# A windowed-attention stage: the sink as one more column of the scores, and two spilled operands split into high and low parts where they are made

## The chip, the cores and the metric

One core of one Trainium2 chip runs the whole program. The metric is the device time of one execution in microseconds: 1199.33 us before the change, the median of 3 runs (1199.18 to 1199.78).

## The reference

One layer of an encoder over 1024 tokens of width 1024, in float32. The part that matters here:

```python
u = rms_norm(h, norm_mix)
z_pool, q, k, v, g_pool, g_attn = split(u @ w_in)      # 512, 512, 128, 128, 1024, 1024 wide
y_pool = (multiscale_pool(z_pool, w_group) * pool_scale) @ w_pool_branch
# attention: 8 query heads, 2 key heads, blocks of 128, each query block sees 3 key blocks
scores = q k^T / 8 - slope_h * |distance|              # -inf beyond distance 128
m = max(max(scores), sink_h)
p = exp(scores - m)
p = p / (sum(p) + exp(sink_h - m))
y_attn = (p @ v) @ w_attn_branch
h = h + (sigmoid(g_pool) * y_pool + sigmoid(g_attn) * y_attn) @ w_out
```

Then a gated feed-forward layer and a last norm, which the change does not touch.

## The kernel before

Every float32 product is made of three matmuls: an operand is split into a rounded high part and the remainder (`hi`, `lo`), and hi\*hi, hi\*lo and lo\*hi are summed. `split` (L85) makes the high part with a cast on ACT (L87) and the remainder with a subtraction on DVE (L88), or on POOL where it is told to.

The input projection is cut in units of 256 columns; each unit takes seven products, P1 to P7 (a Strassen scheme, `product`, L169), of 12 matmuls of 512 columns. Units `z01`, `z23` feed the pooled branch, `kv` and `q01` the keys, values and the first key head's four query heads, `q23` the second key head's four, and `("g", i)` the gates. A gate is passed through a sigmoid (L301) and written to DRAM (`g_dram`, L302). The units `q23`, g6 and g7 are deferred: their products P2 are kept for the attention stage.

The pooled branch: `windows` (L478) makes window means of z, beside the products of the projection, one piece per product; a small product per half of 512 tokens, a scaled copy on ACT (L512), a write to `p_dram` from the POOL queue (L513). `load_branch` (L569) reads it back in four loads of 512 KB into the `raw` tiles that also hold weights, and splits each into `p_hi` and `p_lo` (ACT, and two remainders each on DVE and POOL).

The second key head's queries are written unsplit (`q_dram`, L311), read back by `load_q` (L603) and split by `use_q` (L339): each tile holds a head's high part in one half of the 128 partitions and its remainder in the other, so that one matmul against the keys does both.

The attention stage is a loop (L722 to L746) over 16 units, that is 2 key heads x 8 query blocks. Step i makes the scores of unit i (`scores`, L621), the transposed probabilities of unit i-3 (`probs`, L656), the values of one before (`values`, L670), and between them `STEPS[i]` branch steps (`branch_step`, L692): 12 matmuls of a branch (first `br<-p_hi`, later `br<-a_hi`), times a gate. `LAST` says how many kept products P2 go before a step. A scores unit, of four heads:

```python
tensor_tensor_reduce(out=s, in0=ps, in1=bias, op0=add, op1=max, accum_out=mx)  # DVE L633, per head
negm = min(-mx, nsink)                                                      # DVE L637
se = negm + sink_b; se = exp(se)                                       # DVE L641, ACT L648
s = exp(s + negm), den = its sum                                          # ACT L645, per head
den = den + se; den = 1 / den                                           # DVE L649, L650
s = s * den                                         # L652: heads 1 and 3 on POOL, the rest on DVE
```

What each engine runs in which order is not the order of the code: a scheduler places the instructions of each engine by its own estimate of times. Each engine then runs its list strictly in that order. Every wait is on semaphores. PSUM has 8 banks of 512 columns, the `s` tile has 3 buffers, a gate's tile 4.

Of the kernel before, what the change touches and what calls it, by code (L numbers as in the profile page):

```python
# [39 lines left out]
P_AT = 1  # L40
# [3 lines left out]
P_POOL = ((0, 2), (1, 0))  # L44
WO_TAIL = 3
AB_POOL = 0
Q_POOL = ((1, 0), (0, 1))
Q_AT = (5, 8)
LAST = (0, 3)
# [4 lines left out]
def encoder_kernel(ctx, tc, x, norm_mix, w_in, w_pool_group, pool_scale, sink, w_pool_branch,  # L54
# [20 lines left out]
    q_dram = dram.tile([2 * P, S], F32, name="q_dram")  # L75
    a_dram = dram.tile([512, S], F32, name="a_dram")
    p_dram = dram.tile([512, S], F32, name="p_dram")
# [191 lines left out]
    big = tc.alloc_tile_pool(name="big", bufs=2, side="right")  # L269
    u_rest = tc.alloc_tile_pool(name="u_rest", bufs=1, side="right")  # L270
# [4 lines left out]
    for name in ("S1", "S2", "S3", "S4", "A22"):  # L275
        combos[name] = tuple(u_rest.tile([P, 4, HALF], F32R, name="%s_%s" % (name, p)) for p in ("hi", "lo"))
# [4 lines left out]
    def in_tile(tag, unit):  # L281
        if tag == "c11" and smp_pool:
            return smp_pool[0].tile([P, HALF], F32, tag="ptl", bufs=3, name="c11")
# [12 lines left out]
    def in_result(unit, row, col, src):  # L296
# [9 lines left out]
        elif unit == "q23":  # L306
            out = src
            if (row, col) == (0, 0):
                out = in_tile("c11", unit)
                nc.scalar.copy(out=out, in_=src)  # L310
            nc.gpsimd.dma_start(out=q_dram[col * P:(col + 1) * P, sl], in_=out)  # L311
        elif unit == "q01":
            use_q(col, sl, src)
# [5 lines left out]
    def use_k(sl, src):  # L319

        scale = HD ** -0.5
# [17 lines left out]
    def use_q(j, sl, src, pool=(0, 0)):  # L339
        for i in range(2):  # L340
            own = slice(i * HD, (i + 1) * HD)
            other = slice((1 - i) * HD, (2 - i) * HD)
            q = qq[2 * j + i]
            nc.scalar.copy(out=q[own, sl], in_=src[own])
            (nc.gpsimd if pool[i] else nc.vector).tensor_tensor(
                out=q[other, sl], in0=src[own], in1=as32(q[own, sl]), op=ALU.subtract)
# [103 lines left out]
    nc.vector.tensor_scalar(out=far, in0=dist, scalar1=float(P), scalar2=NEG, op0=ALU.is_gt, op1=ALU.mult)  # L450
# [6 lines left out]
    wg_raw = zp.tile([P, 4, P], F32, name="wg_raw")  # L457
# [20 lines left out]
    def windows(g):  # L478
# [27 lines left out]
        for half in range(2):  # L506
# [11 lines left out]
    for i, (unit, prod) in enumerate(sequence[:-len(deferred)]):  # L518
# [7 lines left out]
        if prod == "P1" and unit == "kv":  # L526
# [9 lines left out]
            for h in range(4):  # L536
                qq[h] = att.tile([P, S], F32R, tag="qq", bufs=4, name="qq")
# [728 lines left out]
```

## Time and profile before

| what | value |
|---|---|
| median of 3 runs | 1199.33 us |
| the profiled execution, its own time | 1198.78 us |
| its span | 1197.0 us |
| PE busy | 1159.4 us, 97% |
| DVE busy | 858.3 us, 72% |
| ACT busy | 542.7 us, 45% |
| POOL busy | 488.5 us, 41% |
| PE's share of the chain that ended last | 86% (DVE 8%, DMA 2%) |
| attention stage within the span | about 284 to 410 us |

An engine's busy time is the time that its instructions cover. PE's matmuls overlap, so a busy PE may still start them further apart than it could. The chain that ended last is followed back from the last instruction, at each step to what released it.

### The profile page before, as it was taken

The page shows a single profiled execution, that of the slowest core. Times are in us where ns is not written, and L with a number is a line of the kernel's source. Part 1 is how long each engine was busy: PE and PEld are TensorE (multiplying, and loading weights), DVE is VectorE, ACT ScalarE, POOL GpSimd, SP SyncE. Part 2 cuts the span into 40 slices and gives each one's busy share as a digit, 9 for nine tenths or more (in the row PEclk, how much of TensorE's full clock was granted, in tenths as well). Part 3 has the DMA queues.
Part 4 walks back from the last instruction along what each step waited for, and adds up shares of the span by engine and source line. Part 5 has one row for each costly group of instructions (what it writes and reads, how often), then busy time and mean ns, then how long its engine had stood idle before and what let it go on. Part 6 is the DMA issues. An engine that isn't in the chain of part 4 may idle for free.

```text
span 1197.0 us, 15588 instructions
## 1 busy us (share of the span) xinstructions
PE 1159.4 (97%) x5284; PEld 958.9 (80%) x5284; DVE 858.3 (72%) x1339; ACT 542.7 (45%) x1044; POOL 488.5 (41%) x429
## 2 busy tenths in 40 slices
PE   7899999999989999999999999999999999999996
PEld 6788888887778878888778888888888878888885
DVE  6954695756999786539868776777767774665774
ACT  6543345535777644447333332332333344454453
POOL 6833353354554552203445544465455620020230
PEclk9999999999999999999999999999999999999998
DMA  6344134126331565626254544545354457755462
GB/s 211 102 128 146 58 103 144 37 96 220 120 105 59 170 199 186 213 86 194 83 190 171 190 141 140 186 167 166 123 195 158 150 189 259 264 190 196 159 234 100
DMA packets 132372, 186.37 MB, mean 156 GB/s; under 512 B 8450, under 2 KB 87298, under 8 KB 132292
## 3 DMA queue, kind: packets, MB, share of 16 engines
q1 hardware_dynamic: 124372, 158.89, 40.6%
q0 software_dynamic: 6480, 21.24, 4.7%
q10 hardware_dynamic: 1440, 5.24, 1.2%
q8 instruction: 41, 0.67, 0.2%
q14 instruction: 39, 0.32, 0.1%
HBM read 133.70 MB, written 51.64 MB: 155 GB/s over the span
## 4 chain that ended last, share of the span: by engine, by line
PE 86%; DVE 8%; DMA 2%; issue 2%; ACT 1%; POOL 0%; SPq 0%; POOLq 0%; DVEq 0%; ACTq 0%
PE dn L825 17%; PE Y L184 15%; PE X L184 14%; PE Z L184 14%; PE W L184 8%; PE wo L978 7%; PE br L216 2%; PE br L217 2%; PE br L215 2%; DVE wlo L88 1%; PE pt L662 1%; DMA sums<-in_w_ffn_down_dram 1%; PE pv L675 1%; PE tp L376 1%; PE pv L676 1%
## 5 line engine op out<-in xcount | busy, mean ns | idle before, releaser
L87 ACT CAST whi<-raw 128x512 fp32r<-128x512 f32 x378 | 231.1, 620 | 349.9 <-POOL raw L145 84.6
L88 DVE TENSOR_TENSOR wlo<-raw,whi 128x512 fp32r<-128x512 f32 x358 | 320.2, 902 | 67.1 <-ACT whi L87 62.1
L145 POOL TENSOR_TENSOR raw<-raw 128x512 f32<-128x512 f32 x140 | 194.9, 1393 | 239.8 <-DVE wlo L88 205.8
L825 PE MATMUL dn<-wlo,ah 128*128 128x512 f32 x308 | 119.8, 389 | 0.4 <-DVE wlo L88 0.4
L825 PE MATMUL dn<-whi,ah 128*128 128x512 f32 x308 | 117.7, 389 | 1.0 <-ACT ah L87 1.0
L825 PE MATMUL dn<-whi,al 128*128 128x512 f32 x308 | 118.2, 389 | 0.0
L88 DVE TENSOR_TENSOR al<-ab,ah 128x512 fp32r<-128x512 f32 x69 | 48.6, 704 | 67.8 <-ACT ah L87 67.7
L87 ACT CAST ah<-ab 128x512 fp32r<-128x512 f32 x69 | 42.9, 622 | 87.9 <-PE dn L825 87.7
L1050 DVE TENSOR_TENSOR sums<-sums 128x256 f32<-128x256 f32 x88 | 51.1, 580 | 35.9 <-DMA sums<-in_w_ffn_down_dram 33.2
L184 PE MATMUL X<-S_hi,whi 128*128 128x512 f32 x192 | 74.8, 390 | 0.0
L184 PE MATMUL X<-S_hi,wlo 128*128 128x512 f32 x192 | 74.7, 389 | 0.0
L184 PE MATMUL X<-S_lo,whi 128*128 128x512 f32 x192 | 74.7, 389 | 0.0
L184 PE MATMUL Z<-a,whi 128*128 128x512 f32 (+1 forms) x240 | 70.5, 379 | 0.0
L184 PE MATMUL Z<-A_hi,whi 128*128 128x512 f32 x176 | 68.7, 390 | 0.0
L184 PE MATMUL Z<-A_lo,whi 128*128 128x512 f32 x176 | 68.7, 390 | 0.0
L825 PEld LDWEIGHTS dn<-whi,ah 128*128 128x128 f32 x308 | 57.8, 188 | 13.5 <-ACT ah L87 1.4
L184 PE MATMUL Z<-A_hi,wlo 128*128 128x512 f32 x176 | 68.5, 389 | 0.0
L825 PEld LDWEIGHTS dn<-wlo,ah 128*128 128x128 f32 x308 | 57.8, 188 | 12.7 <-DVE wlo L88 0.8
L825 PEld LDWEIGHTS dn<-whi,al 128*128 128x128 f32 x308 | 57.8, 188 | 11.9
L652 POOL TENSOR_SCALAR s<-s,den 128x384 f32<-128x384 f32 (+1 forms) x32 | 38.7, 1220 | 44.4 <-DVE den L650 23.1
L184 PE MATMUL W<-S,whi 128*128 128x512 f32 x176 | 55.6, 396 | 1.0 <-ACT S L87 1.0
L1203 POOL TENSOR_TENSOR o<-o,gain_fin 128x512 f32<-128x512 f32 x8 | 12.4, 1568 | 106.1 <-ACT junk L900 106.1
(268 smaller groups left out, 2832.6 us busy)
## 6 DMA issues: line engine op xcount, KB each, us to landing
ab<-act_dram SPq DMA_DIRECT2D x31, 512.0 KB, 4.0
raw<-in_w_in_dram SPq DMA_DIRECT2D x26, 512.0 KB, 3.8
raw<-in_w_ffn_gate_dram SPq DMA_DIRECT2D x22, 512.0 KB, 3.9
raw<-in_w_ffn_up_dram SPq DMA_DIRECT2D x22, 512.0 KB, 3.8
sums<-in_w_ffn_down_dram SPq DMA_DIRECT2D x44, 256.0 KB, 4.5
wt_dram<-sums SPq DMA_DIRECT2D x22, 512.0 KB, 2.8
act_dram<-sums POOLq DMA_DIRECT2D x44, 256.0 KB, 2.9
raw<-wt_dram SPq DMA_DIRECT2D x20, 512.0 KB, 4.5
```

The source lines that it names most:

```text
L87: ins = nc.scalar.copy(out=hi, in_=src)
L88: (eng or nc.vector).tensor_tensor(out=lo, in0=src, in1=as32(hi), op=ALU.subtract)
L145: nc.gpsimd.tensor_tensor(out=out, in0=x0, in1=x1, op=ALU.subtract)
L184: nc.tensor.matmul(ps, wt[:, c], at[:, k, cols], start=opening and k == 0 and i == 0, stop=k == 3 and i == 2, skip_group_check=not opening)
L215: nc.tensor.matmul(ps, wh, xh, start=first, stop=False)
L216: nc.tensor.matmul(ps, wh, xl, start=False, stop=False)
L217: nc.tensor.matmul(ps, wl, xh, start=False, stop=last)
L652: (nc.gpsimd if i in POOL_HEADS else nc.vector).tensor_scalar(out=s[:, i, :W], in0=s[:, i, :W], scalar1=den[:, i:i + 1], scalar2=None, op0 ...
L825: nc.tensor.matmul(ps[t], at[:, ts], wt, start=opening and k == 0 and e == 0, stop=k == nk - 1 and e == 2, skip_group_check=not opening)
L978: nc.tensor.matmul(ps[t], at[:, k, ts], wt, start=k == 0 and e == 0, stop=k == KT - 1 and e == 2)
L1050: nc.vector.tensor_tensor(out=out, in0=in0, in1=in1, op=op)
L1203: nc.gpsimd.tensor_tensor(out=o[t][:, :HALF], in0=o[t][:, :HALF], in1=gain3[:, :HALF], op=ALU.mult)
```

## The change

- The sink becomes one more column of the scores. All scores change their sign (the scale of the keys, the bias and the mask are negated), the reduction takes the minimum, and its start value is the negated sink instead of a constant; so `negm` comes out of the reduction. POOL copies the negated sinks into column W of `s`; the exponential reads W + 1 columns with a scale of -1, and its sum holds the sink's term. L637, L641, L648 and L649 are gone.
- The pooled branch is split when it leaves PSUM (ACT cast with the scale, DVE remainder), both parts are written (`p_dram` has two), and four loads of 1 MB from the ACT queue bring them straight to where the products read them, in the tiles of the projection's operands S1 and S2, which are free by then.
- The second key head's queries are split where they are made too (`q_dram` has two parts), and sixteen loads of 128 KB of 64 partitions each bring the parts to their places. The query tiles are cut in halves of 512 tokens, eight buffers; the second head's tiles reuse the first's.
- The kept products P2 stand before steps 0 (two) and 1 (one) instead of three before step 1. The tiles of `pth` and `ptl` have 4 buffers instead of 3.

```diff
-LAST = (0, 3)
+LAST = (2, 1)
-Q_AT = (5, 8)
+Q_AT = (5, 9)
...
         elif unit == "q23":
-            out = src
             if (row, col) == (0, 0):
-                out = in_tile("c11", unit)
-                nc.scalar.copy(out=out, in_=src)
-            nc.gpsimd.dma_start(out=q_dram[col * P:(col + 1) * P, sl], in_=out)
+                hi, lo = [in_tile("c11", unit).bitcast(F32R) for _ in range(2)]
+            else:
+                hi, lo = in_tile("c11", unit).bitcast(F32R), src.bitcast(F32R)
+            split(src, hi, lo)
+            for i, part in enumerate((hi, lo)):
+                nc.gpsimd.dma_start(out=q_dram[i, col * P:(col + 1) * P, sl], in_=as32(part))
...
-            p = zp.tile([P, HALF], F32, tag="p", bufs=2, name="p")
-            nc.scalar.activation(out=p, in_=ps, func=AF.Copy, scale=psc[:, g:g + 1])
-            nc.gpsimd.dma_start(out=p_dram[g * P:(g + 1) * P, sl], in_=p)
+            hi, lo = [zp.tile([P, HALF], F32, tag="p", bufs=3, name="p").bitcast(F32R) for _ in range(2)]
+            split(ps, hi, lo, scale=psc[:, g:g + 1])
+            for i, part in enumerate((hi, lo)):
+                nc.gpsimd.dma_start(out=p_dram[i, g * P:(g + 1) * P, sl], in_=as32(part))
+    def load_p(half):
+        for i, part in enumerate(("hi", "lo")):
+            p_split[half, i] = t = u_sums.tile([P, 4, HALF], F32R, tag="S%d_%s" % (half + 1, part), bufs=1, name="p_" + part)
+            with tc.issue_after(sigmoids[-1]):
+                nc.scalar.dma_start(out=as32(t),
+                                    in_=p_dram[i, :, half_of(half)].rearrange("(t p) q -> p t q", p=P))
...
+    def load_q(row):
+        for h in range(4):
+            qq[4 + h, row] = q = att.tile([P, HALF], F32R, tag="qq", bufs=8, name="qq")
+            for part, rows in enumerate(rows_of(h % 2)):
+                nc.sync.dma_start(out=as32(q[rows]), in_=q_dram[part, h * HD:(h + 1) * HD, half_of(row)])
...
+        s = sm.tile([P, 4, 3 * P + 8], F32, tag="s", bufs=3, name="s")
+        nc.gpsimd.tensor_copy(out=s[:, :, W], in_=nsink[:, hs])
...
-            nc.vector.tensor_tensor_reduce(out=s[:, i, :W], in0=ps[:, :W], in1=bias[:, i, c0:c0 + W], scale=1.0,
-                                           scalar=NEG, op0=ALU.add, op1=ALU.max, accum_out=mx[:, i:i + 1])
-        ins = nc.vector.scalar_tensor_tensor(out=negm, in0=mx, scalar=-1.0, in1=nsink[:, hs], op0=ALU.mult,
-                                             op1=ALU.min)
-        nc.vector.tensor_tensor(out=se, in0=negm, in1=sink_b[:, hs], op=ALU.add)
+            ins = nc.vector.tensor_tensor_reduce(
+                out=s[:, i, :W], in0=ps[:, :W], in1=bias[:, i, c0:c0 + W], scale=1.0,
+                scalar=nsink[:, 4 * g + i:4 * g + i + 1], op0=ALU.add, op1=ALU.min, accum_out=negm[:, i:i + 1])
...
-                ins = nc.scalar.activation(out=s[:, i, :W], in_=s[:, i, :W], func=AF.Exp, bias=negm[:, i:i + 1],
-                                           accum_out=den[:, i:i + 1])
-        nc.scalar.activation(out=se, in_=se, func=AF.Exp)
-        nc.vector.tensor_tensor(out=den, in0=den, in1=se, op=ALU.add)
+                ins = nc.scalar.activation(out=s[:, i, :W + 1], in_=s[:, i, :W + 1], func=AF.Exp, scale=-1.0,
+                                           bias=negm[:, i:i + 1], accum_out=den[:, i:i + 1])
...
-        if i == P_AT:
-            with behind(P_AT - 1, (0,)):
-                load_branch(p_dram, p_hi, p_lo, pool_t=P_POOL)
```

The lists move where the stage begins. On DVE, before, from the first unit's last reduction on (`sc` is a bank of scores, `p_lo` the pooled branch's remainder):

```order
L633 ISA s,mx<-sc,bias 128x256
L633 ISA mx 128x1
L637 SCALAR_TENSOR_TENSOR negm<-mx,nsink 128x4
L88 TENSOR_TENSOR p_lo<-raw,p_hi 128x2x512 x2
L641 TENSOR_TENSOR se<-negm,sink_b 128x4
L649 TENSOR_TENSOR den<-den,se 128x4
L650 RECIPROCAL den<-den 128x4
L633 ISA s,mx<-sc,bias 128x384
```

And in the change, at the same place:

```order
L646 ISA s,negm<-sc,bias,nsink 128x256
L646 ISA negm 128x1
L656 RECIPROCAL den<-den 128x4
L658 TENSOR_SCALAR s<-s,den 128x256 x2
L646 ISA s,negm<-sc,bias,nsink 128x384
```

Between the first unit's last reduction and the second unit's first, four instructions with a remainder pair of the pooled branch among them are gone.

On ACT, before, at the start of the stage (the sigmoids of the kept products are L301, the exponentials L645):

```order
L301 ACTIVATE s_2411<-s_2411 128x512
L645 ACT_TABLE_LOAD
L645 ACTIVATE s,den<-s,negm 128x256 x4
L648 ACTIVATE se<-se 128x4
L87 CAST whi<-raw 128x512 x2
L301 ACT_TABLE_LOAD
L301 ACTIVATE c_2606<-Z 128x512
L301 ACTIVATE c_2627<-Z 128x512
L310 COPY c_2646<-Z 128x512
L87 CAST whi<-raw 128x512 x2
L87 CAST pth<-pt 128x512 x2
L645 ACT_TABLE_LOAD
```

And in the change, where the loads of the pooled branch's two parts stand too:

```order
L301 ACTIVATE t_2512<-t_2512 128x512
L526 DMA p_hi<-p_dram 128x4x512
L526 DMA p_lo<-p_dram 128x4x512
L84 CAST whi<-raw 128x512
L301 ACTIVATE s_2474<-s_2474 128x512
L84 CAST whi<-raw 128x512 x2
L301 ACTIVATE c_2597<-Z 128x512
L301 ACTIVATE s_2454<-s_2454 128x512
L526 DMA p_hi<-p_dram 128x4x512
L526 DMA p_lo<-p_dram 128x4x512
L84 CAST whi<-raw 128x512
L301 ACTIVATE c_2618<-Z 128x512
```

All sigmoids now stand before the first exponential; the first half's two loads are behind the sigmoid of unit g7's P7, the second half's behind that of its P4.

On SP, before, the loads ahead of the stage (`raw` is the shared tile of weights and spilled parts):

```order
L573 DMA raw<-p_dram 128x2x512 x3
L302 DMA g_dram<-t_2469 128x512
L302 DMA g_dram<-s_2431 128x512
L573 DMA raw<-p_dram 128x2x512
L579 DMA sg<-g_dram 128x512 x4
L104 DMA raw<-in_w_pool_branch_dram 128x4x256
```

And in the change, at the same place:

```order
L101 DMA raw<-in_w_pool_branch_dram 128x4x256 x3
L302 DMA g_dram<-t_2512 128x512
L302 DMA g_dram<-s_2474 128x512
L101 DMA raw<-in_w_pool_branch_dram 128x4x256
L302 DMA g_dram<-c_2597 128x512
L302 DMA g_dram<-s_2454 128x512
L101 DMA raw<-in_w_attn_branch_dram 128x4x256
```

The branch's weights took the place of the spilled parts in the `raw` tiles; the gates' loads moved behind.

On PE, of the change, the list from that P4 (its matmuls are `Y`) to the second branch step runs: 12 `Y`, 13 `Z` (the kept products), 8 `sc` of 256 columns, 12 `Z`, 8 `sc` of 384, 12 `br` (first half of the tokens), 8 `sc`, 8 `pt`, 12 `br` (second half). From there on it repeats 8 `sc`, 12 `pt`, 4 to 6 `pv`, 12 `br`, where before most of these groups were cut in pieces of one to six.

## Rows read from the trace of the kernel before

**Rows 1.** Windows: length, PE, PEld, DVE, ACT, POOL busy (instructions), clock, DMA share, GB/s.

```profile
280.00:420.00 140.00, 132.02 (x683) 111.56 (x682) 126.56 (x337) 99.16 (x243) 75.14 (x58) 0.99 0.41 134
420.00:440.00 20.00, 18.78 (x79) 14.17 (x78) 16.36 (x21) 9.83 (x17) 8.90 (x6) 1.00 0.57 181
284.00:410.00 126.00, 118.02 (x616) 99.91 (x615) 118.81 (x323) 93.34 (x233) 66.73 (x51) 0.99 0.37 122
360.00:410.00 50.00, 50.00 (x274) 43.79 (x273) 45.18 (x132) 35.17 (x91) 22.45 (x18) 1.00 0.31 96
```

**Rows 2.** Timeline of PE, one undisturbed step: start, length, engine, line, instruction, count.

```profile
365.83 0.33 PE L631 MATMUL sc<-kkh,qq 128*128 128x384 f32 x1
...
367.25 1.47 PE L662 MATMUL pt<-ident,s 128*128 128x128 f32 x12
368.48 0.48 PE L675 MATMUL pv<-pth,vv 128*128 128x512 f32 x1
...
369.49 0.39 PE L215 MATMUL br<-p_hi,whi 128*128 128x512 f32 x1
...
372.22 0.33 PE L631 MATMUL sc<-kkh,qq 128*128 128x384 f32 x1
```

**Rows 3.** Waits of PE, 280 to 440 us: us in total, times, longest.

```profile
PE br L215 <- ACT whi L87: 1.6, 1, 1.6
PE sc L631 <- ACT c L301: 1.3, 1, 1.3
```

**Rows 4.** Groups of DVE, 284 to 410 us: busy us, mean ns, idle before.

```profile
L345 DVE TENSOR_TENSOR qq<-raw,qq 64x512 fp32r<-64x512 f32 x4 | 6.1, 1554 | 0.1
L641 DVE TENSOR_TENSOR se<-negm,sink_b 128x4 f32<-128x4 f32 x16 | 5.3, 329 | 0.1
...
L637 DVE SCALAR_TENSOR_TENSOR negm<-mx,nsink 128x4 f32<-128x4 f32 x16 | 4.6, 289 | 0.1
L88 DVE TENSOR_TENSOR p_lo<-raw,p_hi 128x1024 fp32r<-128x1024 f32 x2 | 4.6, 2318 | 0.0
...
L649 DVE TENSOR_TENSOR den<-den,se 128x4 f32<-128x4 f32 x16 | 3.5, 218 | 1.8 <-ACT se L648 1.7
```

**Rows 5.** The instructions of L641 (ns min/median/max), and POOL's timeline at 299 us.

```profile
L641 DVE TENSOR_TENSOR se<-negm,sink_b x16: 135/158/2706, 293.5 to 402.7; 128x4 f32<-128x4 f32 x16
...
299.39 2.51 POOL L88 TENSOR_TENSOR wlo<-raw,whi 128x512 fp32r<-128x512 f32 x2
```

**Rows 6.** Windows around the start of the stage, and the busiest one for DMA.

```profile
296.00:300.00 4.00, 3.15 (x15) 3.06 (x15) 3.93 (x15) 3.34 (x7) 3.97 (x5) 0.70 0.47 177
300.00:304.00 4.00, 4.00 (x19) 3.37 (x18) 4.00 (x8) 3.70 (x9) 1.91 (x2) 0.87 0.49 189
...
280.00:300.00 20.00, 17.11 (x80) 14.36 (x78) 16.44 (x41) 14.51 (x26) 11.70 (x8) 0.94 0.73 246
...
404.00:408.00 4.00, 4.00 (x20) 3.26 (x19) 1.50 (x6) 2.50 (x6) 1.44 (x2) 1.00 1.03 349
```

**Rows 7.** DMA issues: queue, count, KB each, median us from issue to landing.

```profile
p_dram<-p POOLq DMA_DIRECT2D x8, 256.0 KB, 3.2
raw<-p_dram SPq DMA_DIRECT2D x4, 512.0 KB, 3.7
```

**Rows 8.** Windows over the stretch in which the pooled branch is made.

```profile
140.00:200.00 60.00, 60.00 (x264) 49.34 (x263) 47.88 (x66) 28.93 (x47) 30.02 (x25) 1.00 0.35 115
160.00:180.00 20.00, 20.00 (x90) 16.39 (x89) 19.85 (x30) 10.64 (x19) 10.66 (x7) 1.00 0.37 126
200.00:280.00 80.00, 80.00 (x360) 66.38 (x360) 48.92 (x68) 35.18 (x63) 30.91 (x24) 1.00 0.27 83
```

**Rows 9.** Single lines' instructions, ns min/median/max: remainder with a scale, two small POOL operations.

```profile
L328 DVE SCALAR_TENSOR_TENSOR kkl<-Z,kkh x4: 683/688/694, 206.8 to 210.4; 64x512 fp32r<-64x512 f32 x4
...
L476 POOL MEMSET z<- x4: 105/113/115, 58.0 to 140.0; 128x8 f32 x4
...
L908 POOL TENSOR_TENSOR rstd<-ms,mhalf x16: 549/569/1463, 494.2 to 1189.0; 128x1 f32<-128x1 f32 x16
```

More of the change, by code (lines that the diff above doesn't have):

```diff
@@ L39 @@
 FILL = (128, 480)
-P_AT = 1
 BIAS_AT = 5
@@ L269, in encoder_kernel @@
     big = tc.alloc_tile_pool(name="big", bufs=2, side="right")
+    u_sums = tc.alloc_tile_pool(name="u_sums", bufs=1, side="right")
     u_rest = tc.alloc_tile_pool(name="u_rest", bufs=1, side="right")
@@ L275, in encoder_kernel @@
     for name in ("S1", "S2", "S3", "S4", "A22"):
-        combos[name] = tuple(u_rest.tile([P, 4, HALF], F32R, name="%s_%s" % (name, p)) for p in ("hi", "lo"))
+        pool = u_sums if name in ("S1", "S2") else u_rest
+        combos[name] = tuple(pool.tile([P, 4, HALF], F32R, name="%s_%s" % (name, p), tag="%s_%s" % (name, p), bufs=1)
+                             for p in ("hi", "lo"))
     st = tc.alloc_tile_pool(name="st", bufs=1, side="right")
@@ L337, in use_v, with use_q, rows_of @@
             split(pv[:, :, g], vv[0][:, 4 * row:4 * row + 4, g, 0], vv[0][:, 4 * row:4 * row + 4, g, 1])
-    def use_q(j, sl, src, pool=(0, 0)):
+    def use_q(j, row, src):
         for i in range(2):
[L341 to L346, printed above, removed]
+            own, other = rows_of(i)
+            q = qq[2 * j + i, row]
+            nc.scalar.copy(out=q[own], in_=src[own])
+            nc.vector.tensor_tensor(out=q[other], in0=src[own], in1=as32(q[own]), op=ALU.subtract)
+    def rows_of(i):
+        return slice(i * HD, (i + 1) * HD), slice((1 - i) * HD, (2 - i) * HD)
     def in_product(unit, prod, **kw):
@@ L535, in encoder_kernel @@
                 kkl[g] = att.tile([P, S], F32R, tag="kkl", bufs=2, name="kkl")
-            for h in range(4):
-                qq[h] = att.tile([P, S], F32R, tag="qq", bufs=4, name="qq")
+            for row in range(2):
+                for h in range(4):
+                    qq[h, row] = att.tile([P, HALF], F32R, tag="qq", bufs=8, name="qq")
         in_product(unit, prod)
+        if (unit, prod) == (deferred[-1], "P7"):
+            load_p(0)
         ahead(1)
@@ L562, in encoder_kernel @@
     pp = tc.alloc_tile_pool(name="pp", bufs=1, side="right")
-    p_hi, p_lo = [pp.tile([P, 4, S], F32R, name=n) for n in ("p_hi", "p_lo")]
     merged = []
@@ L601, in behind @@
             yield
-    def load_q(h):
-        raw = raw_tile()
-        nc.sync.dma_start(out=raw, in_=q_dram[h * P:(h + 1) * P, :])
-        for i in range(2):
-            qq[4 + 2 * h + i] = (att2 if h == 0 else att).tile([P, S], F32R, tag="qq", bufs=2 if h == 0 else 4,
-                                                             name="qq")
-        for half in range(2):
-            use_q(2 + h, half_of(half), raw[:, half_of(half)], Q_POOL[h])
+    def load_q(row):
+        for h in range(4):
+            qq[4 + h, row] = q = att.tile([P, HALF], F32R, tag="qq", bufs=8, name="qq")
+            for part, rows in enumerate(rows_of(h % 2)):
+                nc.sync.dma_start(out=as32(q[rows]), in_=q_dram[part, h * HD:(h + 1) * HD, half_of(row)])
     sm = tc.alloc_tile_pool(name="sm", bufs=1)
@@ L707, in branch_step @@
             if j == 0:
[L708 removed]
+                load_branch(a_dram, *brs[1:], half)
             held["w"] = weights()
[L710 removed]
+            pool, hi, lo = brs[0], brs[1][:, :, sl], brs[2][:, :, sl]
         gt = load_gate(pool, b * KT + j, half)
[L712 removed]
+        ps = branch(held["w"], hi, lo)
         if b == 0:
@@ L743, in encoder_kernel @@
             if i in Q_AT:
-                with behind(i - 1):
-                    load_q(Q_AT.index(i))
+                load_q(Q_AT.index(i))
             scored.append(scores(g, n, biases[g]))
```

59 lines of the change are left out of this document (25 added, 34 removed).

## The prediction

> **What bounds the kernel now.** I looked first for stretches in which PE is not busy, because the time table shows PE busy for 97% of the span and the chain that ended last is mostly PE. The windows show them in one place: PE is full from 140 to 280 us [rows 8], and between 280 and 420 us it is busy for 132.02 of 140 us [rows 1]. In the same place DVE is at its limit: 118.81 of 126 us between 284 and 410 [rows 1]. PE's waits there [rows 3] name ACT and DVE as releasers, nine short ones of at most 1.6 us, of which two are shown. The change touches nothing else in the kernel but the stretch in which the pooled branch and the queries are made, so the question is how much PE time this stage loses, and how much comes back.
>
> Idle time alone undercounts the loss, because modelled matmuls overlap and because a matmul at half clock counts as busy. So I count what the stage's matmuls need when nothing disturbs them. One such step [rows 2]: 8 score matmuls of 384 columns start within 1.42 us (0.1775 each), 12 transposes within 1.23 (0.1025), 12 matmuls of 512 columns within 2.73 (0.2275), and 4 value matmuls take 1.01, which is 0.1 more than four of 512 columns, so about 0.08 once per unit. For 256 columns I take two thirds of 384, 0.12. The window of 140 us holds 683 matmuls [rows 1]; by the program 176 of them are transposes and 125 are scores as the trace has them (96 of 384, 29 of 256), and 382 have 512 columns. Needed: 382 x 0.2275 = 86.9, 96 x 0.1775 = 17.0, 29 x 0.12 = 3.5, 176 x 0.1025 = 18.0, and 15 x 0.08 = 1.2; together 126.6. **PE loses 13.4 us in 280 to 420.** The next 20 us hold 79 matmuls of 512 columns, 18.0 us of need: 2.0 us lost, where the last attention block goes to DRAM and back before the branch product can read it. Part of the loss is the clock: it stood at 0.70 and 0.87 in two windows of 4 us [rows 6], right after PE had idled, that is 1.2 + 0.5 = 1.7 us of work not done.
>
> **The change part by part.** *The sink column.* DVE loses three small instructions in each of 16 units: 5.3 + 4.6 + 3.5 = 13.4 us [rows 4]. ACT loses 16 small exponentials. The reduction keeps its shape and the exponential reads one column more; nothing for both (were each of the 64 exponentials and 64 reductions 10 ns longer, 0.6 us on engines that then have room). POOL gains 16 copies of 128x4. No row shows one; the nearest are a fill of 128x8 at 0.113 us and a power of 128x1 at 0.569 [rows 9], so 1.8 to 9.1 us, on an engine that is busy for 66.73 of 126 [rows 1]. I take 1.8, since a copy is nearer to the fill. The copy waits until the transposes have left that buffer of `s`, and POOL's normalisations stand behind it; the lag of three units covers that. If the cover went, a step would wait for a copy of up to 0.57 us, 9 us in all.
>
> *The pooled branch.* In the attention stage DVE loses two remainders of 1024 columns, 4.6 us [rows 4], the first of them in front of the second unit's scores, as the lists show; ACT and POOL lose their shares of it. Where the branch is made, DVE gains 8 remainders with a scale, at the 0.688 us of such an instruction of the same length [rows 9]: 5.5 us; ACT keeps its 8 casts. POOL issues 8 writes more. DVE is idle for 12.1 us of 140 to 200 [rows 8], but only for 0.15 between 160 and 180. What hides the 5.5 us are weights split ahead in four buffers; from both sides 0 and 5.5 us of PE, and I take 0.3, by the nearest row: PE is full at 160 to 180 even though DVE is.
>
> *The loads.* Four loads of 1 MB replace four of 512 KB. From the P7 sigmoid to the first use of the second half PE has some 16.5 us of work: 13.0 from the end of the `Y` matmuls (37 of 512 columns 8.4, scores 0.96 + 1.42 + 1.42, transposes 0.82), and about 3.5 before. In 280 to 300 the DMA moved 246 GB/s, 4.9 MB [rows 6], of which one load of 0.5 MB was the pooled branch; that leaves 4.4 in 20 us, 3.6 in 16.5. The new loads add 4.2 MB. The most that any window shows is 349 GB/s [rows 6]. If the four loads go first they need 12.0 us and are in time: 0. If all else goes first, 7.8 MB take 22.4 us: 5.9 us late. Three of the branch's four weight loads (1.5 MB) now stand earlier on the SP queue, as the raw tiles are free: 6.3 MB, 18.1 us, 1.6 late, and with the landing of the last part I take 2.0.
>
> The Trainium skill speaks against the move here, "DMA: Bandwidth & Descriptors", section "Issuing engines are not separate DMA queues": transfers from several engines' queues share the same 16 DMA engines and interleave, so a second queue saves only issue time. No run here has yet shown two queues side by side. With the page's ceiling of about 358 GB/s per core (its section "Specifications") the estimate for 6.3 MB would be 17.6 us, 1.1 late, and the time 0.9 us lower.
>
> *The queries.* In the stage DVE loses 4 remainders, 6.1 us [rows 4], POOL 4 and ACT 8. Where the queries are made, 3 casts and 3 remainders of 512 columns are added; at 0.69 us on DVE they lie in 200 to 280, where DVE is busy for 48.92 of 80 [rows 8]: nothing, and 2.1 us at most without that cover. The fourth pair falls in the stage: 0.7 us of DVE. The 16 small loads stand on the SP queue behind the scores that free their tiles, and gate loads stand behind them. Three units or more pass before the first use of each, so only the gates matter: four gate tiles are in flight, and I put nothing.
>
> *The order.* With all sigmoids before the first exponential, ACT's table is loaded once instead of three times, and PE has two kept products to run while ACT makes the first exponentials, which is where the two waits shown are [rows 3].
>
> **The sum.** DVE in the stage: 118.8 - 13.4 - 4.6 - 6.1 + 0.7 = 95.4 us, against some 113 us of PE work in the same 126 us (126 less the 13 lost). DVE was 6 us over PE's need; now it is 18 under. So PE becomes the bound of this stage and the waits go, except: the pooled loads 2.0; the steps without a branch product, where PE has 4 us of work and DVE 6 (95.4 / 16), 1.0 after what the lag of three covers; 0.3 in the stretch before. The tail keeps 1.7 of its 2.0, because the way to DRAM and back is unchanged. 13.4 - 2.0 - 1.0 - 0.3 + 0.3 = **10.4 us less**. The profiled execution took 1198.78, so 1188.4; it stood 0.55 under the median, so 1188.9 for the median.
>
> **The rivals.** *The pooled loads are late, and the clock falls.* For: 246 GB/s moved there already. Against: the SP queue's gate loads wait for buffers and come late. Price: 5.9 instead of 2.0, and the 1.7 us of clock that came with the idle time before: gain 10.4 - 3.9 - 1.7 = 4.8, time 1194.5.
>
> *DVE is relieved by less.* The small additions of the sink took 158 ns in the median, but 329 in the mean, and one took 2706 while POOL ran two instructions for 2.51 us [rows 5]. So about half of their time was waiting behind POOL, and the next DVE instruction may do that waiting instead. If all of the 24.1 us removed were so, 12 us would stay: DVE 107 of 113. Then half of the waits stay, 6.7, and with the same losses the gain is 3.7: 1195.6.
>
> The Trainium skill has the rule for this, "SBUF — State Buffer", section "Who interferes with whom": a DVE instruction with two SBUF inputs and a GpSimd (POOL) one that reads SBUF exclude each other for the whole instruction. The row of 2706 ns agrees; by the rule the reductions and remainders that read PSUM would not wait in their place, which speaks against this rival.
>
> *The stretch before pays for it: slower.* The pooled branch's `p` tiles are now three, used by pairs, so every remainder writes a tile whose DMA of the half before must have landed, 3.2 us from its issue [rows 7]. DVE is strictly in order: if it waits there, weights and the projection's sums stand behind it. With eight waits of 3.2 and 5.5 us of work, less DVE's 12.1 us of idle time, PE loses 19 us, the stage gives 10.7 back, and the time is 1207.6. It decides the sign from 2.2 us per wait on. Against: the halves lie a product (2.7 us) or more apart, and the lists put other DVE work between.
>
> *The stage is held by its chain, not by DVE.* Scores, exponential, normalisation and transposes follow each other through four engines, and the waits only change their names: about 1199. Against: between 360 and 410, where neither branch nor queries are split, the same chain runs with PE busy throughout [rows 1].
>
> **How the numbers follow.** Forecast 56%, with a range of its own from 1184.9 (all of the 13.4 and half of the tail) to 1193. Late loads 22%, less relief 12%, slower 6%, no change 4%. The range 1184.5 to 1195.5 holds the first two and half of the third. A difference of 0.2%, 2.4 us, is about what a measurement of this kernel can tell from none. Faster by more: 0.56 + 0.22 and half of the third, 0.85. Slower 0.07, the rest 0.08.
>
> **What would show it.** Right: DVE at 93 to 98 us over the stage, PE's waits on DVE gone between 310 and 355, steps of 6.4 to 6.9 us from the third on, one table load. The pooled loads show as PE `br` waiting for a DMA, in the first two branch steps alone. Wrong: DVE below 100 us and the waits still there, with ACT or POOL as releasers; or PE no longer full between 140 and 200 us.

## The result: 1192.17 us, and the profile after

| | before | after |
|---|---|---|
| median of the runs side by side | 1199.55 us | 1192.17 us (1190.59 to 1192.71) |
| ratio | | 0.9936, 95% interval 0.9918 to 0.9953 |
| profiled execution, its span | 1198.78, 1197.0 us | 1191.99, 1190.1 us |

The change is 7.4 us faster; 10.4 were forecast, and the time lies in the range.

To see where the 6.9 us of span came from, fixed points are better than windows of fixed times, because later work moves into those. I take the last matmul of the projection (`Y`) and the last one of the attention branch (`br<-a_hi,wlo`). From PE's timeline of the kernel before, and then of the change (start, length, line, instruction):

```profile
283.77 0.39 PE L184 MATMUL Y<-A_hi,wlo 128*128 128x512 f32 x1
...
453.50 0.39 PE L217 MATMUL br<-a_hi,wlo 128*128 128x512 f32 x1
```

```profile
285.11 0.39 PE L181 MATMUL Y<-A_hi,wlo 128*128 128x512 f32 x1
...
446.04 0.39 PE L214 MATMUL br<-a_hi,wlo 128*128 128x512 f32 x1
```

The **stage** between them took 169.73 us and takes 160.93: 8.80 less. The way to its start is 1.34 us longer, and from its end to the end of the span it is 743.50 before and 744.06 after, 0.56 longer. -8.80 + 1.34 + 0.56 = -6.90. The windows of just this stage, before and then after (columns as in [rows 1]):

```profile
284.16:453.89 169.73, 160.53 (x803) 133.76 (x802) 155.75 (x372) 113.28 (x266) 93.12 (x69) 0.99 0.44 141
```

```profile
285.50:446.43 160.93, 157.16 (x802) 133.61 (x802) 138.67 (x319) 99.80 (x235) 85.58 (x80) 0.99 0.53 170
```

PE does nearly the same work (803 and 802 matmuls recorded), but not the same matmuls: 7 more of 512 columns and 6 fewer short scores fall into the stage before, since the lists place some of each ahead of its start. By the prices of the prediction the stage's matmuls need 154.4 us before and 153.5 in the change. So PE loses 15.4 us in it before and 7.4 after: 8.0 of the 8.80 are won, and 0.9 is work that now stands ahead of the start, which is most of the 1.34. DVE is busy for 17.1 us less in it, ACT 13.5, POOL 7.5, and the DMA moves more. The windows of the change that answer to [rows 1, 6, 8]:

```profile
280.00:420.00 140.00, 136.98 (x718) 117.95 (x717) 115.40 (x291) 89.50 (x217) 72.59 (x73) 0.99 0.51 165
420.00:440.00 20.00, 19.25 (x83) 14.89 (x82) 18.22 (x23) 11.14 (x19) 9.05 (x7) 1.00 0.71 230
284.00:410.00 126.00, 122.98 (x656) 106.36 (x655) 107.40 (x279) 83.09 (x207) 66.71 (x68) 0.99 0.52 168
...
140.00:200.00 60.00, 59.75 (x262) 48.79 (x261) 55.13 (x75) 28.13 (x46) 30.90 (x32) 1.00 0.39 139
...
288.00:292.00 4.00, 4.00 (x23) 3.43 (x23) 2.42 (x10) 3.67 (x8) 3.16 (x3) 1.00 1.06 400
292.00:296.00 4.00, 4.00 (x21) 3.53 (x20) 3.12 (x9) 3.12 (x10) 2.87 (x3) 1.00 1.06 407
296.00:300.00 4.00, 2.84 (x19) 2.45 (x17) 3.13 (x12) 1.90 (x6) 3.73 (x5) 1.00 1.06 400
300.00:304.00 4.00, 2.58 (x8) 2.05 (x9) 2.40 (x7) 2.88 (x10) 1.41 (x3) 0.77 0.86 325
304.00:308.00 4.00, 4.00 (x22) 3.60 (x21) 1.71 (x5) 1.59 (x4) 2.95 (x3) 0.80 0.22 77
```

PE's idle time is now nearly all at one place, 296 to 308 us, and the waits of 280 to 440 (us in total, times, longest) name it. Of the nine before, beside the two of [rows 3]:

```profile
PE pv L675 <- DVE merged L714: 1.3, 1, 1.3
PE pt L662 <- DVE ptl L88: 1.2, 1, 1.2
PE pv L675 <- DVE mx L633: 1.2, 1, 1.2
PE br L215 <- ACT a_hi L87: 0.9, 1, 0.9
PE sc L631 <- DVE at L683: 0.7, 1, 0.7
PE sc L631 <- DVE qq L345: 0.4, 1, 0.4
PE br L216 <- DVE a_lo L88: 0.3, 1, 0.3
```

In the change those on `a_hi` and `a_lo`, in the tail, are left of them; the late load is new, and two more of 0.2 us are not shown:

```profile
PE br L213 <- DMA p_lo<-p_dram: 2.6, 1, 2.6
PE br L212 <- ACT a_hi L84: 0.5, 1, 0.5
PE br L213 <- DVE a_lo L85: 0.3, 1, 0.3
```

The second branch step waits for the remainders of the second half; then the granted clock is 0.77 and 0.80 in two windows of 4 us, that is for a part of them 1.2 instead of 2.4 GHz; (0.23 + 0.20) x 4 = 1.7 us of work not done. The DMA issues of 276 to 312 us (queue, count, KB each, median us to landing; the second `p_lo` alone also took 14.7):

```profile
p_hi<-p_dram ACTq DMA_DIRECT2D x2, 1024.0 KB, 9.8
p_lo<-p_dram ACTq DMA_DIRECT2D x2, 1024.0 KB, 14.7
```

In the groups of DVE, 284 to 410 us, the small instructions, the branch's two remainders and the queries' four [rows 4] are gone, but the reduction has become longer. Before, and then now:

```profile
L633 DVE CUSTOM_DVE_ANT_0 s<-sc,bias 128x384 f32<-128x384 f32 x48 | 24.6, 549 | 0.1
L633 DVE CUSTOM_DVE_ANT_0 s<-sc,bias 128x256 f32<-128x256 f32 x16 | 5.8, 413 | 0.0
```

```profile
L646 DVE CUSTOM_DVE_ANT_0 s<-sc,bias,nsink 128x384 f32<-128x384 f32 x48 | 27.3, 609 | 3.2 <-PE sc L645 3.2
...
L646 DVE CUSTOM_DVE_ANT_0 s<-sc,bias,nsink 128x256 f32<-128x256 f32 x16 | 6.8, 477 | 0.0
```

And the added instructions, POOL's copy and the remainder with a scale (ns min/median/max), beside [rows 9]:

```profile
L639 POOL COPY s<-nsink x16: 180/191/536, 286.9 to 385.0; 128x4 f32<-128x4 f32 x16
...
L88 DVE SCALAR_TENSOR_TENSOR p<-gm,psc,p x8: 732/741/752, 152.3 to 199.3; 128x512 fp32r<-128x512 f32 x8
```

### The profile page after: what moved, and what is told of

Read it like the earlier page. It is cut to its first block, busy times and chain, and to the rows that moved or that the text cites. A ratio compares the mean times of both kernels' runs of the same rounds, so it can differ in the third digit from the quotient of the medians.

```text
span 1190.1 us, 15576 instructions
## 1 busy us (share of the span) xinstructions
PE 1154.1 (97%) x5284; PEld 955.8 (80%) x5284; DVE 854.1 (72%) x1297; ACT 531.2 (45%) x1017; POOL 485.0 (41%) x451
## 4 chain that ended last, share of the span: by engine, by line
PE 80%; DVE 10%; DMA 4%; issue 3%; ACT 1%; POOL 1%; SPq 0%; POOLq 0%; DVEq 0%; ACTq 0%
PE dn L827 17%; PE X L181 13%; PE Y L181 13%; PE Z L181 12%; PE wo L980 7%; PE W L181 7%; DVE wlo L85 3%; PE br L213 2%; PE br L214 2%; PE br L212 2%; DMA sums<-in_w_ffn_down_dram 2%; DMA p_lo<-p_dram 1%; PE pt L668 1%; PE pv L681 1%; PE pv L682 1%
## 5 line engine op out<-in xcount | busy, mean ns | idle before, releaser
L827 PEld LDWEIGHTS dn<-whi,ah 128*128 128x128 f32 x308 | 57.8, 188 | 13.5 <-ACT ah L84 1.4
```

The source lines that it names most:

```text
L827: nc.tensor.matmul(ps[t], at[:, ts], wt, start=opening and k == 0 and e == 0, stop=k == nk - 1 and e == 2, skip_group_check=not opening)
```

## The experiments

Beside the times I give each run's stage, read between the same two matmuls as above; it repeats better than the time (the change in two profiled executions 160.93 and 160.67, its improved version 157.96 and 157.95), while the rest of the span scatters: from the stage's end on it took 742.6 to 744.9 us in these profiles. Every other kernel's stage is one profiled execution. Since not quite the same matmuls lie between the two fixed ones everywhere, the table also gives what PE loses in it, that is the stage less its matmuls by the prices of the prediction, and DVE's busy time in it, all in us:

| kernel | stage | PE's loss | DVE busy |
|---|---|---|---|
| before | 169.73 | 15.4 | 155.75 |
| sink_only | 168.88 | 14.5 | 149.32 |
| q_only | 170.17 | 15.8 | 146.68 |
| q_last21 | 163.98 | 10.3 | 141.86 |
| p_only | 167.58 | 14.1 | 147.84 |
| the change | 160.93 | 7.4 | 138.67 |
| change_side | 160.67 | 7.2 | 139.79 |
| no_sink | 160.85 | 7.4 | 143.54 |
| last03 | 162.95 | 8.8 | 141.76 |
| buf3 | 165.25 | 11.8 | 137.99 |
| p_early | 159.18 | 5.1 | 140.63 |
| early_nosink | 160.00 | 6.0 | 143.99 |
| early_const | 157.96 | 3.9 | 137.26 |
| early_side | 157.95 | 3.7 | 137.29 |

### The parts one by one

**sink_only**: the kernel before with the sink as a column, and nothing else.

```diff
-            mx = reduce(ps + bias, max); negm = min(-mx, nsink); se = exp(negm + sink_b); den = den + se
+            negm = reduce(ps + bias, min, start nsink); column W of s = nsink; the exponential reads W + 1
```

> The kernel before with the sink column alone (signs, seed, copy, exponential); pooled branch and queries are loaded and split as before. Theory A (DVE's length of the attention stage decides, each part counts by what it takes off DVE): the three small instructions take 13.4 us off DVE, the reductions get 64 x 0.06 = 4 us longer, so 9 us net of the 118.8; PE's waits from 310 to 355 us shrink, those at 292 to 297 stay, because the pooled remainders still stand in front of the second unit: 2 to 4 us less than before, 1195.5 to 1197.5. Rival B (the pooled branch and the queries made nearly all of the loss): within 1 us of before. Rival C (the small instructions, which also wait behind POOL, made it): 7 us less, as the whole change.

1197.86 us, ratio 0.9981 (0.9970 to 0.9992), stage 168.88. DVE busy for 111.99 of 284 to 410 us instead of 118.81. It helps a little by itself: 2.3 us in the medians, as theory A had it, but only 0.9 of PE's loss in its profiled stage; the rest is not found there.

**no_sink**: the change with the sink as before.

> The changed kernel with the old sink: maximum with a constant start, three small DVE instructions and one exponential more per unit, no copy. Theory A: DVE gains 13.4 - 4 = 9 us in the stage and is again near PE's need, so some short waits come back in steps that carry no branch product and around the second bias: 1 to 3 us more than the changed kernel, 1193.2 to 1195.2. Rival B: within 1 us of the changed kernel. Rival C: back to before, 1198 to 1199.

1192.86 us, ratio 0.9938 (0.9921 to 0.9956), stage 160.85: the change's own. DVE has 113.09 us of work between 284 and 410 instead of 107.40 and the time is the same. **On top of the other parts, with the late load, the sink column is worth nothing.** Something is traded all the same: PE's wait for `p_lo` is 0.9 us here instead of 2.6, and waits on DVE have come, 1.1 for `merged` and 0.6 for `s`. What the column is worth with the load in time, the last runs show.

**q_only**: the kernel before with the queries split where they are made.

```diff
-            nc.gpsimd.dma_start(out=q_dram[col * P:(col + 1) * P, sl], in_=out)
+            split(src, hi, lo)
+            for i, part in enumerate((hi, lo)):
+                nc.gpsimd.dma_start(out=q_dram[i, col * P:(col + 1) * P, sl], in_=as32(part))
```

> The kernel before with the queries alone split where they are made and loaded in sixteen pieces into halved tiles. Theory A: 6.1 us less on DVE, in two bursts at 325 and 347 us; the waits next to them (0.4 and 1.3 us, and their restarts) go: 1 to 3 us less than before, 1196.5 to 1198.5. Rival B': the queries cost nothing where they were: within 0.7 us of before.

1201.56 us, ratio 1.0013 (1.0003 to 1.0023), stage 170.17: slower, a miss. The waits of 325 to 350 us are gone as expected, but new ones stand at the start. ACT's, DVE's and PE's timelines there:

```profile
294.97 1.14 ACT L87 CAST whi<-raw 128x512 fp32r<-128x512 f32 x2 [4.16 <-DMA raw<-in_w_pool_branch_dram]
```

```profile
296.13 6.26 DVE L618 SCALAR_TENSOR_TENSOR bias<-dist 128x384 f32<-128x384 f32 x4 [9.06 <-ACT whi L87]
```

```profile
296.83 0.44 PE L632 MATMUL sc<-kkh,qq 128*128 128x384 f32 x1 [2.85 <-ACT c L301]
302.79 0.69 PE L632 MATMUL sc<-kkh,qq 128*128 128x384 f32 x1 [4.58 <-DVE mx L634]
```

ACT stands behind a late load of weights; DVE stands for 9.06 us in front of the first write of `bias`, and the bias then takes 6.26 us for four instructions whose median is 552 ns, while POOL runs remainders from SBUF (2.82 us from 295.67, 2.49 from 299.01). The Trainium skill, "SBUF — State Buffer", section "Who interferes with whom", says that a DVE instruction with two SBUF inputs and a POOL one reading SBUF exclude each other; this row agrees with it. As what released the `bias` the row names ACT's cast; in the list as built the `bias` waits for an earlier sigmoid and for three DMA queues, and the write `g_dram<-s`, issued at 291.39, took 4.6 us to land, so it is the likelier one.

**q_last21**: q_only with the kept products in the change's places.

```diff
-LAST = (0, 3)
+LAST = (2, 1)
```

> The kernel before with the queries' split alone (as q_only), but with the kept products two before step 0 and one before step 1. Theory M (q_only lost only by an accident of the lists at the start: ACT stood 4.2 us behind a late load of branch weights, DVE 9.1 us behind ACT, and PE 7.4 us behind both; the queries' own worth, the waits of 325 to 350 us, is there and shows as soon as PE has other work): 1195 to 1197.5, with under 3 us of PE waits between 290 and 306 us. Rival N (one split alone cannot pay, because the other still fills DVE at the start): 1199 to 1202, with 5 us or more of PE waits there.

1195.30 us, ratio 0.9952 (0.9935 to 0.9969), stage 163.98. The time is as theory M said, its bound on the waits is not: PE still waits 3.0 and 2.8 us there. DVE stood nearly as long as in q_only:

```profile
293.16 1.97 DVE L618 SCALAR_TENSOR_TENSOR bias<-dist 128x384 f32<-128x384 f32 x4 [8.46 <-DMA g_dram<-s]
```

So rival N's time falls, though its waits came: the queries pay without the pooled branch, 5.75 us of stage together with the order (5.1 of PE's loss). That it is the two kept products which cover DVE's stand is argued from their place.

**p_only**: the kernel before with the pooled branch split where it is made, loaded ready, and the kept products at (2, 1).

```diff
-            nc.scalar.activation(out=p, in_=ps, func=AF.Copy, scale=psc[:, g:g + 1])
-            nc.gpsimd.dma_start(out=p_dram[g * P:(g + 1) * P, sl], in_=p)
+            split(ps, hi, lo, scale=psc[:, g:g + 1])
+            for i, part in enumerate((hi, lo)):
+                nc.gpsimd.dma_start(out=p_dram[i, g * P:(g + 1) * P, sl], in_=as32(part))
```

> The kernel before with two parts of the change: the pooled branch split where it is made and loaded ready, and the kept products in the change's places (two before step 0, one before step 1). The queries and the sink stay as before. Theory E (the pooled branch carries the gain: without its loads, casts and remainders at the start of the stage PE's waits of 290 to 320 us shrink, and the queries' remainders later only cost the waits that the kernel before had at 325 to 350): 1193 to 1195, that is 5 to 7 us less than before. Rival F (the two splits must come together, since either alone leaves DVE above 100 us in the stage and the lists only put the waits elsewhere, as the queries alone did): 1198 to 1201, no more than 2 us from before.

1197.92 us, ratio 0.9982 (0.9967 to 0.9996), stage 167.58, at the edge of rival F. It trades one wait for another: 3.2 us for `p_lo`, where casts and remainders were waited for.

With the order, then, p_only gives 2.15 us of stage (1.3 of PE's loss) and q_last21 5.75 (5.1), and both together 8.88 (8.0, no_sink). The sum is not a test of whether the two splits help or hinder each other: the order is counted in both runs, and both have three buffers for `pth` and `ptl` where no_sink has four, which buf3 shows to count for more than the difference. Of the two runs the queries' gives more, also with the stand of DVE that it has and the change has not. How the 5.75 divides between the order and the queries stays open: without it the queries gave nothing (q_only), and the order alone on the kernel before was not run.

### What the change does beside its parts

**last03**: the change with the kept products where they were.

```diff
-LAST = (2, 1)
+LAST = (0, 3)
```

> The change with the kept products where they were before: three before step 1, none before step 0. Theory G (the kept products before step 0 fill the time in which the first exponentials and the table load run; without them PE waits there, and after the wait it runs at half clock): 2 to 4 us more than the change, 1194.5 to 1196.5, with a PE wait on ACT or DVE of 1.5 us or more between 288 and 298 us. Rival H (the start is bound by the pooled loads, so work moved behind them gives them time: the wait for p_lo shrinks as the other grows): within 1 us of the change, 1191.5 to 1193.

1193.94 us, ratio 0.9951 (0.9934 to 0.9968), stage 162.95, 2.0 longer than the change's (1.4 of PE's loss). The time lies between theory G's 1194.5 and rival H's 1193. No wait is where theory G put one: the only long one is 1.8 us for `p_lo`, less than the change's 2.6 as rival H had it, and the rest of the loss is spread.

**buf3**: three buffers for the transposed probabilities instead of four.

```diff
-            hi = smp.tile([P, 512], F32R, tag="pth", bufs=4, name="pth")
-            lo = smp.tile([P, 512], F32R, tag="ptl", bufs=4, name="ptl")
+            hi = smp.tile([P, 512], F32R, tag="pth", bufs=3, name="pth")
+            lo = smp.tile([P, 512], F32R, tag="ptl", bufs=3, name="ptl")
```

> The change with three buffers instead of four for the high and low parts of the transposed probabilities. Theory O (these buffers are a silent part of the gain, and the reason why the two splits together give more than the sum of them apart, which ran with three): 1194.5 to 1197, with PE's transposes or scores waiting for DVE ptl or ACT pth at 1 us or more in all. Rival P (the splits themselves make the gain): within 1 us of the change.

1197.51 us, ratio 0.9979 (0.9969 to 0.9988), stage 165.25. The size is near theory O's, half a microsecond above its range; the mechanism isn't: no PE wait names `pth` or `ptl`. The loss is at the start; DVE's timeline, then PE's:

```profile
295.30 0.69 DVE L85 TENSOR_TENSOR c<-Z,c 128x512 fp32r<-128x512 f32 x1 [6.92 <-ACT c L84]
298.05 1.97 DVE L628 SCALAR_TENSOR_TENSOR bias<-dist 128x384 f32<-128x384 f32 x4 [2.06 <-DMA g_dram<-s]
```

```profile
300.48 0.68 PE L212 MATMUL br<-p_hi,whi 128*128 128x512 f32 x1 [3.82 <-DVE negm L646]
```

DVE's list now has a query's remainder ahead of the bias, and the bias waits for a gate's write to DRAM. The lists as built show the difference: in the change (first line) the `bias` has no wait, with three buffers it waits for three DMA queues.

```
L628 SCALAR_TENSOR_TENSOR bias<-dist 128x384 x4
L628 SCALAR_TENSOR_TENSOR bias<-dist 128x384 [waits DMAHW1_49,DMAHW5_49,DMASW5_49,DVE_49]
```

q_only and q_last21, also with three, stand in front of the same instruction; the kernel before and p_only, with three too, don't. My reading is that the sizes of the tiles decide whose memory `bias` takes over, and the scheduler then reorders around the wait. The addresses in the programs as built agree in all six. In buf3, q_only and q_last21 the first `bias` starts at byte 112128 of a partition and so reaches 2 KB into the pool of the projection's `s1` tiles (105984 to 114176); in the change (116224), the kernel before and p_only (120320) it lies beyond. The wait is for that whole pool: the write to DRAM that ends it reads another of its tiles (105984 to 108032), while the 2 KB that `bias` takes were last used well before. So what pays is where `bias` lies, and not that a fourth buffer of `pth` or `ptl` is used. One step stays argued: a kernel with three buffers and other memory for `bias` was not tried.

### The late loads, and the longer reduction

**p_early**: the change with the pooled loads issued a few products sooner.

```diff
-        if (unit, prod) == (deferred[-1], "P7"):
-            load_p(0)
+        if (unit, prod) in ((deferred[-1], "P5"), (deferred[-1], "P6")):
+            load_p(int(prod == "P6"))
...
-    load_p(1)
```

> The changed kernel with the pooled branch's loads issued as soon as their tiles are free: first half after unit g7's P5, second after its P6, where the change issues them after P7 and after P4 (some 9 and 12 us earlier). Theory A (the second half's low part is late, since the DMA is full at 400 GB/s from 284 to 300 us, and the half clock after it is its consequence): PE's wait of 2.6 us and the 1.6 us at half clock go: 4 us less than the changed kernel, 1188. Rival D (the DMA is full whatever goes first: then gates or weights of the branch are late in place of it): within 1 us of the changed kernel, with a new wait of br for weights or of the gate product for a gate.

1190.87 us, ratio 0.9924 (0.9904 to 0.9944), stage 159.18, 1.75 less than the change's (2.3 of PE's loss). The time is neither theory A's 1188 nor, by 0.3, rival D's "within 1 us". The wait for the DMA and the half clock are gone, but part of what they cost comes back at once as other waits:

```profile
PE sc L643 <- DVE ptl L85: 0.9, 1, 0.9
PE pv L680 <- DVE merged L720: 0.6, 1, 0.6
```

**early_nosink**: p_early with the sink as before.

> p_early with the sink as in the kernel before: no column, the maximum, and the four small instructions per unit back. Theory K (with the loads in time DVE has room in the stage, so its 13 us of small instructions cost nothing): within 0.7 us of p_early, 1190.2 to 1191.6. Rival L (with the loads out of the way DVE's length counts again, and the sink column is worth what it is worth on the kernel before): about 2 us more, 1192.5 to 1193.5.

1190.80 us, ratio 0.9926 (0.9911 to 0.9941), stage 160.00: 0.8 us of stage for the sink column, and no difference in the time. Theory K for the time.

**early_const**: p_early with a constant start for the minimum. The sink then acts in the sum alone; the quotient is the same, as long as no sink lies so far above all scores that its exponential overflows.

```diff
-                scalar=nsink[:, 4 * g + i:4 * g + i + 1], op0=ALU.add, op1=ALU.min, accum_out=negm[:, i:i + 1])
+                scalar=-NEG, op0=ALU.add, op1=ALU.min, accum_out=negm[:, i:i + 1])
```

> The change with the pooled loads earlier (first half behind P5 of the last unit, second half behind P6), as in p_early, and with the reduction's start value a large constant instead of the negated sink; the sink then takes part in the sum alone, which gives the same quotient. Theory I (the start value read per partition is what made the 64 reductions 60 ns longer): the 384-column reduction falls from 609 to about 549 ns, DVE loses 4 us in the stage, and since DVE is no longer what ends PE's waits the time moves by at most 1 us against p_early: 1190 to 1191. Rival J (the longer row of s or the minimum makes it longer): 609 ns stay, and the time is that of p_early, 1190.9, within 0.5.

1190.09 us, ratio 0.9921 (0.9906 to 0.9935), stage 157.96. Its reductions (ns min/median/max over both widths), where the change's are 466/607/618:

```profile
L645 DVE CUSTOM_DVE_ANT_0 s<-sc,bias x64: 409/546/558, 291.2 to 391.2; 128x384 f32<-128x384 f32 x48, 128x256 f32<-128x256 f32 x16
```

Theory I: the start value read per partition, not the minimum or the longer row, costs 60 ns. The time is 0.8 us below p_early's, as theory I allowed, the stage 1.2: with the loads in time PE's waits at the start name DVE, and p_early's wait for `ptl` falls from 0.9 to 0.2. **So the column in this form is worth 2.0 us of stage against early_nosink** (0.7 in the medians, whose ranges overlap), where in no_sink it was worth nothing. PE is nearly full there:

```profile
280.00:300.00 20.00, 20.00 (x102) 17.23 (x100) 12.00 (x30) 12.03 (x28) 10.62 (x13) 1.00 0.97 359
300.00:320.00 20.00, 19.48 (x103) 15.88 (x102) 19.91 (x56) 13.82 (x37) 10.49 (x11) 1.00 0.69 220
```

**change_side and early_side**: the change and early_const on one chip, five rounds.

> The change itself, beside early_side on one chip. If the pooled loads' lateness costs what the loss by place says (2.8 us of wait and 1.6 us of half clock), this is 2 to 3 us above early_side; if later waits in the transition to the feed-forward layer give it back, less than 1 us.

> The best version so far (early_const), beside the change on one chip: 1189.5 to 1190.5, against 1192 to 1192.7 for the change.

1192.93 (1191.58 to 1194.74) and 1189.88 us (1189.24 to 1191.60); ratios to before 0.9940 (0.9926 to 0.9954) and 0.9915 (0.9900 to 0.9930). The medians are 3.1 us apart, 2.7 of them in the stage (160.67 and 157.95). This is the best version: 10.0 us faster than the kernel before.

## Why the prediction was right, and where it was off

**The bound: PE took over, but not by DVE's sum of work.** PE's waits on DVE between 310 and 355 went, from 319.91 to 333.59 two steps take 6.84 us each, within the forecast of 6.4 to 6.9, and one table load is left (289.44). But the prediction set DVE's total against PE's, and the total does not decide. The stages of no_sink and buf3:

```profile
286.29:447.14 160.85, 156.77 (x802) 132.00 (x802) 143.54 (x367) 101.87 (x251) 82.83 (x64) 1.00 0.52 171
287.65:452.90 165.25, 158.44 (x802) 133.19 (x802) 137.99 (x319) 99.50 (x235) 84.79 (x80) 0.99 0.50 165
```

buf3 has 5.6 us less of DVE work and a stage 4.4 longer, since DVE stands in front of one instruction at its start. What counts is what stands ahead of what on DVE's list. The forecast for 280 to 440 was 10.7 less, that is 4.7 of loss left of 15.4; 7.4 are left in the stage.

**DVE's relief was overstated.** 24.1 - 0.7 = 23.4 us were to go. Over the stage it was 17.1. The step that failed is "the reduction keeps its shape ... nothing": 27.3 + 6.8 - 24.6 - 5.8 = 3.7 us more (early_const shows the cause). 2.6 more did not go, because a group's time cannot be taken off a busy time: the groups overlap, since an instruction starts before the one ahead of it has ended. In the stage their lines add up to 175.8 us for 155.75 busy, and to 154.3 for 138.67 after: 21.5 less by groups, 17.1 by busy time. The sign of being right, 93 to 98 us in 284 to 410, did not come: 107.40. That also forgot that a shorter stage lets later work into a fixed window: 656 matmuls for 616.

**The late loads: about 2.0, by errors that cancel.** The wait is 2.6 and 1.7 of work is missing at the half clock, as the first rival had it, but removing both gave 1.75 us of stage, 2.3 of PE's loss (p_early), since other waits came up. The half clock shows no price of its own: in change_side, the same kernel, the wait is 2.1 us, the clock stays full, and the stage is only 0.26 shorter.

```profile
300.00:304.00 4.00, 1.90 (x14) 1.56 (x14) 3.41 (x11) 2.05 (x7) 3.28 (x4) 1.00 1.07 404
```

The working was off: I took 246 GB/s as what there is and 349 as the most [rows 6]. But that is not the busiest window of the kernel before. One of the same length shows 411:

```profile
504.00:508.00 4.00, 4.00 (x27) 3.46 (x25) 2.99 (x4) 3.15 (x7) 2.94 (x2) 1.00 1.05 411
```

In the change the queues moved 400 to 407 from 288 to 300 us, and 10.19 MB in 276 to 312. At 400 the 6.3 MB of the sum take 15.8 of the 16.5 us: the sum would have said in time. The transfer was late all the same because the sum let all four loads go at once, while the second half's low part is issued at 286.67, behind sigmoids on ACT's list, and shares the DMA with the weights, gates and queries; issued sooner, it is in time (p_early). On its own queue it took 14.7 us for 1 MB at a full DMA. The rule of the Trainium skill that I had weighed, "DMA: Bandwidth & Descriptors", section "Issuing engines are not separate DMA queues", that queues of several engines share the same 16 DMA engines, agrees with this. The ceiling of about 358 GB/s in "Specifications" on that page of the Trainium skill does not hold for these rows.

**Steps and tail.** Priced at 1.0 for the steps and 1.7 for the tail. The change has only waits of 0.2 us or less from 313 to 420; in the tail the waits named are 0.5 and 0.3, and 1.0 to 1.3 for `a_hi` in change_side, early_const and early_side. In the change 7.4 - 2.6 - 1.7 = 3.1 us are lost beside the late load, near the 2.7. But the terms do not simply add: without the late load the rest is 5.1 (p_early), and 3.9 with the constant start.

**The stretch before.** 0.3 forecast; the windows show 0.25 us of PE idle in 140 to 200 us [rows 8], a wait on `wlo` of 0.2 us. DVE's work there rose by 7.2 us, 5.9 of them the 8 remainders (0.741 us each where 0.688 was taken). No wait on the `p` tiles' DMA was there, so the rival that ended slower fell. The stage starts 1.34 us later all the same, 0.9 of it by the matmuls that now stand ahead of its start. The rest is within the scatter: the last `Y` starts at 285.11 in the change and at 288.06 in change_side, the same kernel, and in sink_only, which has nothing of this part, at 285.58 against 283.77.

**The rivals.** "DVE relieved by less" was right that some stays, and wrong that PE pays for it: no_sink, with the small instructions back (4.9 us more of busy DVE in its stage), has the change's stage. "Held by its chain" fell with the steps.

**What the prediction left out.** It priced the fourth buffer at nothing by not mentioning it, and it is worth 4.3 us of stage (buf3). With three the same change takes 1197.51 us, above the range that was given, though DVE is relieved as much: that the time came out in the range is in part luck. It named the order of the kept products only as cover for two waits; it is worth 2.0 in the change (1.4 of PE's loss) and 6.2 with the queries alone (5.5; q_only against q_last21). And it valued the three parts by their DVE time; by that measure the sink (13.4 us) was the largest, and on top of the others, as it was made, it adds nothing.

## What to carry to other kernels

A saving counts only where something waits for it, so price parts one after another, not by their sum of busy time: the sink column was worth nothing behind a late load, 0.8 us of stage once the load was in time, and 2.0 with a constant start value. When an engine runs its list in order, ask what stands in front of the first instruction of a new stage: a tile that takes over memory of an earlier pool can make the whole engine wait for the last transfer of that pool, and a change of one buffer elsewhere can decide it. Issue a load where its data and its tile are ready, not where its reader is near: a few products earlier, and a constant start value, gave 3 us more here.

## What the runs showed of the hardware

- A reduction with a start value read per partition takes 609 ns for 384 columns and 477 for 256; with a constant 548 and 417.
- DRAM and SBUF exchanged 400 to 407 GB/s on one core in three windows of 4 us running, on two hardware queues (288 to 300 us of the change); the kernel before shows 411 in one such window (504 to 508) on a single hardware queue.
- After PE had waited 2.6 us at one place the granted clock stood at 0.77 and 0.80 in the next two windows; after 3.8 us (buf3) at 0.58; after 1.8 us (last03, its window 300 to 304) at 0.66; after 2.1 us (change_side) it stayed at 1.00. So the length of the one wait alone does not order these rows.
- POOL's copy of 128x4 into a strided column took 191 ns in the median, 536 at most.
